# A hybrid decoder block on one core: value blocks read out behind the next split, and a bias operand of 128 rows instead of 48

## The chip, the cores and the metric

The kernel runs on one core of a Trainium2 chip. The metric is device time in microseconds (us) of one execution; lower is better. Unless marked ns, every time below is in us. A core has TensorE (matmuls, and weight loads that overlap them), VectorE, ScalarE, GpSimd and SyncE; the last one here issues most of the loads. In rows of the profile they are called PE (its weight loads PEld), DVE, ACT, POOL and SP. L454 is line 454 of the kernel before.

## The reference, cut to what matters

One layer, 256 tokens, width 2048, float32. The input is normalised to h and multiplied by one wide weight matrix `w_in`; four branches (causal pooling, dilated window attention, gated linear attention, cross-attention into 256 memory tokens) work on slices of the product. Sigmoid gates of the same product weigh the branches, and a projection with a norm and a residual ends the layer.

```
h = rms_norm(x, g_pre)
proj = h @ w_in                               # 2048 x 19472
(a_val, a_gate, sq, sk, sv, s_gate, cq, ck, cv, c_gate, c_lr,
 mq, m_gate, g_logits) = split(proj)
y_a = pool_mixer(a_val, a_gate, ...)
y_b = swa_mixer(sq, sk, sv, s_gate)
y_c = gla_mixer(cq, ck, cv, c_lr, c_gate, ...)   # gated linear attention
y_m = mem_attn(mq, m_gate, mem, ...)
gates = sigmoid(g_logits.reshape(B, S, 4, 2048) + b_merge)
merged = sum over the branches b of gates[:, :, b] * (y_b @ w_br_b)
x = x + rms_norm(merged @ w_out, g_post)
```

Two pieces of this are touched. `cv` (1024 columns) together with `c_lr` (16 columns) is the value projection of the linear attention. `b_merge` (4 x 2048) is the bias of the gates.

## The kernel before, in words

**Products in three matmuls.** Each float32 operand is split into a high half (rounded to fp32r) and a low half (the remainder). `split_w` (L149 to L154) does it for a stretch of weights: ScalarE copies the raw weights into the high tile (L152), VectorE subtracts to get the low tile (L153). `mm3` (L156 to L160) then multiplies high by high, high by low and low by high. TensorE therefore waits for both engines at the start of a stretch, and ScalarE comes first.

**Blocks.** `b_unit` computes 128 output columns of a projection, `a_block` up to 512 columns for both halves of the tokens. An `a_block` takes two accumulators in PSUM, walks four units of weights (each a DMA by SyncE into a raw buffer, L146, then one or two splits and their matmuls), and returns `finish`, which reads the two accumulators out. It has a parameter `late`: if it is given, it is called directly behind the block's first split and under `behind()`, which puts each instruction it makes behind that split on the same engine. The output projection at the kernel's end uses `late` with accumulators that alternate between two sets of buffers (`acc` and `seven`); other blocks call `finish` at once.

**The value blocks.** `cv` with `c_lr` is 1040 columns wide and done in three blocks of 348, 346 and 346 columns (`CV_BLOCKS`). All three use the set `acc`, which has two buffers: a block takes both. `cv_evac` (L546 to L554) reads them out with ScalarE copies (L550). Between one block's matmuls and the next one's stand whatever gate matmuls the gate stream puts there.

**The gate stream.** The 8192 gate columns are the kernel's largest product. `all_gates` is a generator; `gates(work)` is called after each stretch of the other blocks and advances it by as much work as was done (times 1.13), so that gate matmuls lie between the others. `gate_pair` computes 1024 of these columns with a scheme that needs fewer products. Twice in each pair an accumulation begins with `bias` (L454): one matmul whose moving operand is `brow`, 48 rows of which rows 0 to 15 hold the 16 rows of 512 bias values (high halves) and rows 32 to 47 their low halves, with zeros between. Its stationary operand is one column of `sel`, broadcast to 128 columns, that picks one row of the sixteen (or the sum of two). There are eight gate pairs and sixteen such matmuls. `bias_prep` (L434 to L451) fills `brow` and `sel` once.

**Order.** Dependencies and buffers are tracked by the framework in which the kernel is written. It also settles the order of each engine's instructions when the kernel is built, by priority (the code's order) and by what it expects to be ready; so an engine's order is not everywhere that of the code. Once built, each engine runs its list in order. `behind()` adds an edge that this ordering must keep.

Of the kernel before, what the change touches and what calls it, by code (L numbers as in the profile page):

```python
# [9 lines left out]
R = mybir.dt.float32r  # L10
AF = mybir.ActivationFunctionType
ALU = mybir.AluOpType
AX = mybir.AxisListType

P = 128
# [22 lines left out]
def kernel(ctx, tc, ins, out):  # L38
    nc = tc.nc
    ten, vec, act, pool, sync = nc.tensor, nc.vector, nc.scalar, nc.gpsimd, nc.sync  # L40

    cst = ctx.enter_context(tc.tile_pool(name="cst", bufs=1))
# [5 lines left out]
    def e8(name, shape, dt=F32):  # L48
        return big.tile(shape, dt, tag="e8", bufs=NB_E8, name=name)
# [4 lines left out]
    def c2(name, shape, dt=F32):  # L54
        return big.tile(shape, dt, tag="c2", bufs=NB_C2, name=name)
# [4 lines left out]
    def acc(name, shape):  # L60
        return ps.tile(shape, F32, tag="acc", bufs=2, name=name)

    def seven(name):
        return ps.tile([P, 512], F32, tag="seven", bufs=4, name=name)
# [13 lines left out]
    def behind():  # L78

        stack = ExitStack()  # L80
        for i in last_split:
            stack.enter_context(tc.issue_after(i))
        return stack
# [7 lines left out]
    def pull(n):  # L91
        while n > 0 and queue:
            if step(queue[0][1]):
                queue.pop(0)
            else:
                n -= 1
# [12 lines left out]
    def gates(work):  # L109
        if gate_stream[0] is None:  # L110
            return
        credit[0] += GATE_SHARE * work
        while credit[0] > 0 and gate_stream[0] is not None:
            try:
                credit[0] -= next(gate_stream[0])
            except StopIteration:
                gate_stream[0] = None
# [14 lines left out]
    ident = cst.tile([P, P], F32, name="ident")  # L132
# [11 lines left out]
    def load_raw(src, n):  # L144
        raw = new_raw()
        sync.dma_start(raw[:, :n], src[:, :n])  # L146
        return raw

    def split_w(raw_ap, n, name):  # L149
        hi = wp.tile([P, 1024], R, tag="hi", bufs=NB_HILO, name=name + "h")  # L150
        lo = wp.tile([P, 1024], R, tag="lo", bufs=NB_HILO, name=name + "l")
        last_split[0] = act.activation(hi[:, :n], raw_ap, AF.Copy).ins  # L152
        last_split[1] = vec.tensor_tensor(lo[:, :n], raw_ap, hi[:, :n].bitcast(F32), op=ALU.subtract).ins  # L153
        return hi, lo  # L154

    def mm3(o, sh, sl, wh, wl, start=False, stop=False, again=False):  # L156

        ten.matmul(o, lhsT=sh, rhs=wh, start=start, stop=False, skip_group_check=again)  # L158
        ten.matmul(o, lhsT=sh, rhs=wl, start=False, stop=False, skip_group_check=again)  # L159
        ten.matmul(o, lhsT=sl, rhs=wh, start=False, stop=stop, skip_group_check=again)  # L160

    def a_block(name, units, stat, nw, evac, load=None, per_split=None, other=False, late=None):

        accs = [seven(f"{name}a{t}") if other else acc(f"{name}a{t}", [P, 512]) for t in range(2)]
        nk = 4 * len(units)
        for u, src in enumerate(units):
            raw = load_raw(src, 4 * nw) if load is None else load(u, src)
            nk_s = max(1, 1024 // nw) if per_split is None else per_split(u)
            for hf in range(4 // nk_s):
                hi, lo = split_w(raw[:, hf * nk_s * nw : (hf + 1) * nk_s * nw], nk_s * nw, f"{name}{u}{hf}")  # L170
                if late is not None:
                    with behind():
                        late()
                    late = None
                for t in range(2):
                    ts = slice(t * P, (t + 1) * P)
                    for kk in range(nk_s):
                        k = 4 * u + nk_s * hf + kk
                        ws = slice(kk * nw, (kk + 1) * nw)
                        sh, sl = stat(k)  # L180
                        mm3(accs[t][:, :nw], sh[:, ts], sl[:, ts], hi[:, ws], lo[:, ws], k == 0, k == nk - 1)
                if hf % 2 == 0:
                    pull(1)
                gates(nk_s * 6 * (nw / 2.4 + 14) * 1e-3)
            pull(1)

        def finish():
            for t in range(2):
                evac(t, accs[t][:, :nw])

        return finish
# [5 lines left out]
    def b_unit(name, src, mov, evac, ready=None):  # L197

        a = acc(f"{name}a", [P, 512])
        if ready is None:  # L200
            raw = load_raw(src, 2048)
        for hf in range(2):
            hi, lo = ready[hf] if ready else split_w(raw[:, hf * 1024 : (hf + 1) * 1024], 1024, f"{name}{hf}")
            for kk in range(8):
                k = 8 * hf + kk
                ws = slice(kk * P, (kk + 1) * P)
                mh, _ = mov(k)
                ten.matmul(a[:], lhsT=hi[:, ws], rhs=mov.both(k), start=(k == 0), stop=False)
                ten.matmul(a[:, :T], lhsT=lo[:, ws], rhs=mh, start=False, stop=(k == KT - 1))
            if hf == 0:  # L210
                pull(1)
                gates(2.8)
        if pinned[0]:
            with behind():
                evac(name, a)
        else:
            evac(name, a)
        pull(1)
        gates(2.8)
# [30 lines left out]
    def hilo_tiles(name):  # L250
        hl = [e8(f"{name}hl{i}", [P, 4, 2, T], R) for i in range(4)]

        def at(k):
            return hl[k // 4][:, k % 4, 0, :], hl[k // 4][:, k % 4, 1, :]

        at.both = lambda k: hl[k // 4][:, k % 4]
        at.four = lambda c, i: hl[c][:, :, i, :]
        return at
# [51 lines left out]
    h_at = hilo_tiles("x")  # L310
# [114 lines left out]
        return sh[:, t * P : (t + 1) * P], sl[:, t * P : (t + 1) * P]  # L425


    brow = cst.tile([48, 512], R, name="brow")
    sel = cst.tile([48, 24], R, name="sel")

    walpha = cst.tile([16, 512], F32, name="walpha")
    big_cst = cst.tile([P, 1344], F32, name="big_cst")
# [1 line left out]
    def bias_prep():  # L434
        pool.tensor_copy(walpha[:, 0:1], xcol[0:16, 0:1])
        pool.tensor_copy(big_cst[:, 0:1], xcol[:, 0:1])
        pool.dma_start(walpha[:], ins["w_alpha"])
        pool.dma_start(big_cst[:], ins["consts"])
        raw = c2("braw", [48, 512])
        pool.memset(raw[:], 0.0)  # L440
        rows = ins["b_merge"].rearrange("b (j c) -> (b j) c", c=512)
        pool.dma_start(raw[0:16, :], rows)
        pool.dma_start(raw[32:48, :], rows)
        act.activation(brow[:], raw[:], AF.Copy)
        vec.tensor_tensor(brow[32:48, :], raw[32:48, :], brow[32:48, :].bitcast(F32), op=ALU.subtract)
        one = c2("bsel", [48, 24])
        vec.tensor_tensor(one[:, 0:16], ident[0:48, 0:16], ident[0:48, 32:48], op=ALU.add)
        two = one[:, 0:16].rearrange("p (r i) -> p r i", i=2)
        vec.tensor_tensor(one[:, 16:24], two[:, :, 0], two[:, :, 1], op=ALU.add)
        vec.tensor_copy(sel[:], one[:])  # L450
        yield  # L451

    def bias(o, r):
        ten.matmul(o, lhsT=sel[:, r : r + 1].to_broadcast([48, P]), rhs=brow[:], start=True, stop=False)  # L454

    gate_dram = {}

# [83 lines left out]
    cv = e8("cv", [P, 2, 1024])  # L541
# [4 lines left out]
    def cv_evac(j):  # L546
        def evac(t, a):
            c0, n = CV_BLOCKS[j]
            nv = min(n, 1024 - c0)
            act.activation(cv[:, t, c0 : c0 + nv], a[:, :nv], AF.Copy)  # L550
            if nv < n:
                act.activation(lr[:, t, :], a[:, nv:n], AF.Copy)

        return evac  # L554
# [136 lines left out]
    for n in range(8):  # L691
        if n == 6:
            drain("quarters")
            pinned[0] = False
            gate_stream[0] = all_gates()
        if n < 6:
            ahead[cqk[n + 1][0]] = b_split(*cqk[n + 1])
        evac = plain_evac(gq[:, n, :], SCALE) if n < 4 else plain_evac(gk[:, n - 4, :])
        b_unit(*cqk[n], h_at, evac, ahead.pop(cqk[n][0], None))
    for j in range(3):  # L700
        c0, n = CV_BLOCKS[j]
        a_block(f"cv{j}", [ins[f"w_cv{j}"][u] for u in range(4)], h_at, n, cv_evac(j))()
    queue.append(("mnorm", m_norm()))
    queue.append(("gla", gla()))
    for h in range(4):
# [109 lines left out]
    for g in (3, 2, 1, 0):  # L815
        u = c4(f"u{g}", [P, 2, PAD + T])
# [127 lines left out]
    for n, (j, i) in enumerate(order):  # L944
        name, b, nu = branches[i]
# [35 lines left out]
    late = None  # L981
    for j in range(3):
        late = a_block(f"o{j}", [ins["w_out"][j, u] for u in range(4)], o_at, 512, o_evac(j, 512 * j, 512),
                       other=j % 2 == 1, late=late)
# [5 lines left out]
    for u in range(4):  # L990
        raw = load_raw(ins["w_last"][1, u], 1024)
# [104 lines left out]
```

## Time and profile before

| what | value |
|---|---|
| three runs | 1174.86 median, 1171.3 to 1175.29 |
| the profiled execution | 1172.68, of which its span 1170.6 |
| clock granted to TensorE | 0.998 of full speed |
| HBM | 285.11 MB read, 17.83 MB written, 259 GB/s over the span |
| gate weight loads (`in_w_g`) | 112 loads of 1024 KB, median 5.8 from issue to landing |
| value block loads (`in_w_cv`) | 12 loads, 3.9 to 6.9 from issue to landing |

A row of the timeline gives start, duration, engine, line, operation, output <- inputs and count; in brackets stand the idle time of the engine just before it and what ended that. Matmuls are pipelined, so a matmul's duration is longer than its share of TensorE's time: the step from one start to the next is what it takes. A row of the waits gives who waited for whom, in total, how often, and the longest. A row of one line's instructions gives minimum, median and maximum duration in ns and the first and last start. A row of groups gives the count, then busy time in us and the mean of one in ns, then the idle time before.

### The profile page before, as it was taken

To read this page: it belongs to the slowest core of one execution; us is meant where nothing else is said; L and a number is where in the kernel's file an instruction comes from. 1 tells how busy PE (TensorE), PEld (TensorE's weight loads), DVE (VectorE), ACT (ScalarE), POOL (GpSimd) and SP (SyncE) were. 2 spreads that over 40 slices of the span, in tenths; PEclk is the share of its full clock that TensorE was granted. 3 is DMA by queue.
4 is the path that set the end of the run, shared out by engine and by line. 5 is a ranking of instruction groups with operands and counts; after the bars stand their busy time and mean duration, and the time that the engine had idled before them with its cause. 6 is when DMAs were issued, how large, how long until landed. Compare 5 with 4: busy or idle time off the path is not lost.

```text
span 1170.6 us, 15411 instructions
## 1 busy us (share of the span) xinstructions
PE 1149.8 (98%) x5854; PEld 968.2 (83%) x5854; DVE 961.2 (82%) x1201; ACT 647.0 (55%) x823; POOL 59.0 (5%) x109
## 2 busy tenths in 40 slices
PE   9999999999999999999999999999999999999997
PEld 7887898878888888878888887888788888888887
DVE  7979798999898799889989988987898676777454
ACT  7656456665655555665566556566555543434441
POOL 0010000000101001000000000000000102110000
PEclk9999999999999999999999999999999999999999
DMA  9755679757868688777788777876778988759321
GB/s 356 316 182 193 217 251 343 277 203 281 304 238 284 217 297 289 259 251 263 276 295 315 251 263 271 294 253 231 272 252 303 372 308 306 252 206 381 118 73 73
DMA packets 79946, 303.94 MB, mean 260 GB/s; under 512 B 6224, under 2 KB 8656, under 8 KB 57344
## 3 DMA queue, kind: packets, MB, share of 16 engines
q1 hardware_dynamic: 65568, 268.45, 63.5%
q0 software_dynamic: 8976, 24.91, 6.1%
q10 hardware_dynamic: 5328, 9.60, 2.2%
q8 instruction: 46, 0.75, 0.3%
q14 instruction: 28, 0.23, 0.1%
HBM read 285.11 MB, written 17.83 MB: 259 GB/s over the span
## 4 chain that ended last, share of the span: by engine, by line
PE 76%; DVE 5%; DMA 3%; ACT 2%; issue 2%; DVEq 0%; POOLq 0%; POOL 0%; ACTq 0%
PE q L158 5%; PE q L159 5%; PE q L160 5%; DMA raw<-in_w_g 2%; PE p L158 2%; PE p L159 1%; PE p L160 1%; PE sv2a L159 1%; PE sv0a L158 1%; PE sv0a L160 1%; PE o0a L160 1%; PE sv2a L158 1%; PE o0a L158 1%; PE sv1a L158 1%; PE sv0a L159 1%
## 5 line engine op out<-in xcount | busy, mean ns | idle before, releaser
L491 DVE TENSOR_TENSOR raw<-raw 128x1024 f32<-128x1024 f32 x64 | 78.1, 1220 | 8.9 <-DMA raw<-in_w_g 8.9
L497 DVE TENSOR_TENSOR raw<-raw 128x512 f32<-128x512 f32 x64 | 44.5, 696 | 1.1
L492 DVE TENSOR_TENSOR raw<-raw 128x512 f32<-128x512 f32 x64 | 44.5, 697 | 0.5
L918 POOL DMA_DIRECT2D g<-gd x32 | 17.4, 554 | 98.6 <-DVE merged L926 66.7
L926 DVE TENSOR_TENSOR merged<-merged,g 128x512 f32<-128x512 f32 x24 | 15.5, 686 | 0.0
L710 POOL DMA_DIRECT2D cgd<-cgate x4 | 2.2, 552 | 201.7 <-DVE cgate L241 201.7
L885 POOL DMA_DIRECT2D ybd<-ybt x4 | 2.7, 678 | 174.1 <-DVE ybt L247 174.1
L853 PE MATMUL sp<-k,q 128*128 128x128 f32 (+1 forms) x48 | 10.2, 335 | 1.0 <-DVE k L226 1.0
L861 ACT ACTIVATE s<-s,st 128x384 f32<-128x384 f32 (+1 forms) x8 | 6.2, 769 | 6.7 <-DVE st L860 6.7
L853 PEld LDWEIGHTS sp<-k,q 128*128 128x128 f32 x48 | 7.4, 190 | 2.9 <-DVE k L226 1.4
L856 DVE SCALAR_TENSOR_TENSOR s<-big_cst,sp 128x128 f32<-128x128 f32 (+1 forms) x24 | 7.1, 349 | 2.0 <-PE sp L853 2.0
L246 ACT ACTIVATE xhl<-xn 128x1024 fp32r<-128x1024 f32 x4 | 4.2, 1060 | 7.0 <-DVE xn L330 7.0
L459 ACT ACTIVATE c<-c 128x512 f32<-128x512 f32 x8 | 5.0, 628 | 5.5 <-DVE c L505 3.9
L939 ACT ACTIVATE mTh<-mtp 128x512 fp32r<-128x512 f32 x8 | 4.3, 595 | 6.3 <-PE mtp L937 6.3
L459 ACT ACTIVATE c<-p 128x512 f32<-128x512 f32 x8 | 4.7, 587 | 5.1 <-PE p L160 5.1
L664 POOL TENSOR_TENSOR ms<-ms,half 128x2 f32<-128x2 f32 x4 | 5.7, 1428 | 35.2 <-DVE ms L663 35.2
L879 PE MATMUL po<-pt,sv 128*128 128x256 f32 x24 | 7.2, 384 | 0.2 <-ACT pt L874 0.2
L812 POOL DMA_DIRECT2D yad<-yat x4 | 2.7, 686 | 88.5 <-DVE yat L247 88.5
L360 DVE SCALAR_TENSOR_TENSOR mhl<-mr,vecs,mhl 128x256 fp32r<-128x256 f32 x16 | 6.8, 479 | 0.4 <-issue 0.3
L652 POOL TENSOR_TENSOR sq<-sq 128x256 f32<-128x256 f32 x4 | 4.4, 1106 | 53.0 <-ACT sq L651 53.0
L359 ACT ACTIVATE mhl<-mr,vecs 128x256 fp32r<-128x256 f32 x16 | 6.9, 495 | 0.2 <-DMA mr<-in_memT 0.2
L1003 POOL TENSOR_TENSOR opart<-opart,half 128x1 f32<-128x1 f32 x2 | 1.1, 562 | 116.0 <-DVE opart L1002 116.0
(4603 smaller groups left out, 4582.7 us busy)
## 6 DMA issues: line engine op xcount, KB each, us to landing
raw<-in_w_g SPq DMA_DIRECT2D x112, 1024.0 KB, 5.8
raw<-in_w_sqk SPq DMA_DIRECT2D x24, 1024.0 KB, 6.6
raw<-in_w_sv SPq DMA_DIRECT2D x12, 1024.0 KB, 6.5
raw<-in_w_out SPq DMA_DIRECT2D x12, 1024.0 KB, 9.6
raw<-in_w_cqk SPq DMA_DIRECT2D x8, 1024.0 KB, 15.0
raw<-in_w_cg SPq DMA_DIRECT2D x8, 1024.0 KB, 6.6
raw<-in_w_av SPq DMA_DIRECT2D x8, 1024.0 KB, 5.0
raw<-in_w_ag SPq DMA_DIRECT2D x8, 1024.0 KB, 6.0
```

Of the source, the lines that this page charges most:

```text
L158: ten.matmul(o, lhsT=sh, rhs=wh, start=start, stop=False, skip_group_check=again)
L159: ten.matmul(o, lhsT=sh, rhs=wl, start=False, stop=False, skip_group_check=again)
L160: ten.matmul(o, lhsT=sl, rhs=wh, start=False, stop=stop, skip_group_check=again)
L459: act.activation(dst, src, AF.Tanh, scale=0.5)
L491: vec.tensor_tensor(r4[:, :, 0, :], r4[:, :, 0, :], r4[:, 1, :, :], op=ALU.add)
L492: vec.tensor_tensor(r4[:, 1, 1, :], r4[:, 1, 1, :], r4[:, 0, 0, :], op=ALU.add)
L497: vec.tensor_tensor(r4[:, 0, 1, :], r4[:, 0, 1, :], r4[:, 1, 1, :], op=ALU.add)
L853: ten.matmul(parts[g], lhsT=q3[:, g, it * P : (it + 1) * P], rhs=k3[:, g, :nj], start=True, stop=True)
L856: vec.scalar_tensor_tensor(s[:, g, :], dist[:, g, :], SLOPES[g * 4 + hh], parts[g], op0=ALU.mult, op1=ALU.add)
L879: ten.matmul(po[:], lhsT=sv[g][:, 0, vs], rhs=pt[g][:, 0:T], start=(g == 0), stop=False)
L918: pool.dma_start(gs[t][:], gate_dram[b, j, t][:])
L926: vec.tensor_tensor(m, m, gs[t][:], op=ALU.add)
```

## The change

Two parts. The `finish` of a value block is no longer called at once: it goes into the next block as `late`, and so stands behind that block's first split on ScalarE; the third one's is called behind the loop. The tiles of the bias grow from 48 to 128 partitions; rows 48 to 127 are zero, and the bias matmul has 128 rows.

```
-    brow = cst.tile([48, 512], R, name="brow")
-    sel = cst.tile([48, 24], R, name="sel")
+    brow = cst.tile([P, 512], R, name="brow")
+    sel = cst.tile([P, 24], R, name="sel")
...
-        raw = c2("braw", [48, 512])
+        raw = c2("braw", [P, 512])
         pool.memset(raw[:], 0.0)
...
-        one = c2("bsel", [48, 24])
-        vec.tensor_tensor(one[:, 0:16], ident[0:48, 0:16], ident[0:48, 32:48], op=ALU.add)
+        one = c2("bsel", [P, 24])
+        vec.tensor_tensor(one[:, 0:16], ident[:, 0:16], ident[:, 32:48], op=ALU.add)
...
     def bias(o, r):
-        ten.matmul(o, lhsT=sel[:, r : r + 1].to_broadcast([48, P]), rhs=brow[:], start=True, stop=False)
+        ten.matmul(o, lhsT=sel[:, r : r + 1].to_broadcast([P, P]), rhs=brow[:], start=True, stop=False)
...
+    late = None
     for j in range(3):
         c0, n = CV_BLOCKS[j]
-        a_block(f"cv{j}", [ins[f"w_cv{j}"][u] for u in range(4)], h_at, n, cv_evac(j))()
+        late = a_block(f"cv{j}", [ins[f"w_cv{j}"][u] for u in range(4)], h_at, n, cv_evac(j), late=late)
+    late()
```

## Prediction

> **What bounds the kernel now.** I read the engines' busy times and the chain that ended last first.
>
> ```profile
> PE 1149.8 (98%) x5854; PEld 968.2 (83%) x5854; DVE 961.2 (82%) x1201; ACT 647.0 (55%) x823; POOL 59.0 (5%) x109
> PE 76%; DVE 5%; DMA 3%; ACT 2%; issue 2%; DVEq 0%; POOLq 0%; POOL 0%; ACTq 0%
> ```
>
> TensorE is busy for 98% of the span and carries three quarters of the chain. Only two things can shorten this kernel: an idle stretch of TensorE that goes, or a matmul that takes less of TensorE's time. The change tries one of each, so the next view is who TensorE waits for (in total, how often, the longest).
>
> ```profile
> PE p L158 <- ACT p1c L480: 2.4, 4, 0.9
> PE cv1a L158 <- ACT cv100h L152: 1.2, 1, 1.2
> PE p L159 <- DVE gu2100l L153: 0.6, 1, 0.6
> PE cv1a L159 <- DVE cv100l L153: 0.3, 1, 0.3
> ```
>
> The longest single wait is the start of the second value block, and the DVE wait that follows it belongs to the same place. Idle time is one thing; a busy TensorE can also be slow. So I then looked at the timeline around the bias matmuls, because a step from one start to the next shows what a matmul really takes.
>
> ```profile
> 607.51 0.39 PE L159 MATMUL q<-gv0131l,quarter 128*128 128x512 f32 x1
> 607.74 0.39 PE L160 MATMUL q<-gv0131h,quarter 128*128 128x512 f32 x1
> 608.06 0.50 PE L454 MATMUL p<-brow,sel 48*128 48x512 f32 x1
> 608.49 0.50 PE L158 MATMUL p<-gu1100h,xhl 128*128 128x512 f32 x1
> 608.83 0.40 PE L159 MATMUL p<-gu1100l,xhl 128*128 128x512 f32 x1
> ```
>
> Two ordinary matmuls of 512 columns start 0.23 apart (607.51 to 607.74). Around the bias the steps are 0.32, 0.43 and 0.34. The bias starts late, its successor starts late, and so does the one after.
>
> **First part: the value blocks read out behind the next split.** The seam between the first and the second value block, in the timeline of ScalarE, of VectorE and of TensorE:
>
> ```profile
> 139.66 0.46 ACT L550 ACTIVATE cv<-cv0a 128x348 f32<-128x348 f32 x1 [5.11 <-PE cv0a L160]
> 140.60 0.46 ACT L550 ACTIVATE cv<-cv0a 128x348 f32<-128x348 f32 x1 [0.48 <-PE cv0a L160]
> 140.96 0.77 ACT L152 ACTIVATE cv100h<-raw 128x692 fp32r<-128x692 f32 x1
> ```
>
> ```profile
> 141.76 0.88 DVE L153 TENSOR_TENSOR cv100l<-raw,cv100h 128x692 fp32r<-128x692 f32 x1 [5.66 <-ACT cv100h L152]
> ```
>
> ```profile
> 140.09 0.32 PE L159 MATMUL cv0a<-cv031l,xhl 128*128 128x348 f32 x1
> 140.25 0.32 PE L160 MATMUL cv0a<-cv031h,xhl 128*128 128x348 f32 x1
> 141.78 0.59 PE L158 MATMUL cv1a<-cv100h,xhl 128*128 128x346 f32 x2 [1.22 <-ACT cv100h L152]
> 142.70 0.42 PE L159 MATMUL cv1a<-cv100l,xhl 128*128 128x346 f32 x1 [0.33 <-DVE cv100l L153]
> ```
>
> ScalarE waited 5.11 for the block's sums, copied both accumulators, and only then began the split that TensorE needs. VectorE had nothing for 5.66. The change moves that split (one ACT instruction of 0.77) ahead of the two copies; nothing is added or removed, and the load of the split's data is issued where it was. So the question is when the data is there: the issue in SyncE's timeline, and the DMA list of this stretch with the median time to landing.
>
> ```profile
> 135.34 1.12 SPq L146 DMA_DIRECT2D raw<-in_w_cv  x2
> ```
>
> ```profile
> raw<-in_w_cv SPq DMA_DIRECT2D x2, 692.0 KB, 4.5
> ```
>
> The first of these two loads goes out at 135.34; with the 4.5 median to landing it is there at about 139.8 (an estimate). The split then starts 1.1 earlier than 140.96. Its low half starts at about 140.65 instead of 141.76, and the first product with that half at about 141.6 instead of 142.70. An earlier landing gives up to the time at which the old block itself ends. The matmul that starts at 142.70 is the third after the one at 140.25, and with no wait it would come at 140.25 + 3 x 0.16 = 140.73 with no wait, so the seam can give back at most 1.97. (0.16 is the step from 140.09 to 140.25.) I take 1.4, nearer to what the landing allows, and keep 0 and 2.0 as ends.
>
> What comes late next? The accumulators. All three blocks use the same two, so the first matmul of the second block now waits for a copy that stands behind the split: 139.8 + 0.77 + 0.46 = 141.0, still before the low half is ready. The second copy can't start before 140.60, as now, and ends at 141.06; its matmuls come after six others. So this wait stays hidden, by some tenths. On ScalarE the splits of the block's second half and of the gate weights are queued behind the waiting copies. They are now queued there as well, and VectorE, which works without a break afterwards, moves forward with the first low half.
>
> The second seam shows the asked-for order already, because the instruction order is settled when the kernel is built and need not be the code's:
>
> ```profile
> 163.00 0.77 ACT L152 ACTIVATE cv200h<-raw 128x692 fp32r<-128x692 f32 x1
> 163.68 0.44 ACT L550 ACTIVATE cv<-cv1a 128x346 f32<-128x346 f32 x1
> 164.01 0.77 ACT L152 ACTIVATE cv201h<-raw 128x692 fp32r<-128x692 f32 x1
> ```
>
> ```profile
> 163.88 0.32 PE L160 MATMUL cv1a<-cv131h,xhl 128*128 128x346 f32 x1
> 164.04 0.39 PE L158 MATMUL q<-gt006ah,quarter 128*128 128x512 f32 x1
> ...
> 166.76 0.32 PE L158 MATMUL cv2a<-cv200h,xhl 128*128 128x346 f32 x1
> ```
>
> Split, copy, split; TensorE goes straight on with a gate's matmuls (starts 0.16 apart, then 0.23). Nothing is to be had there: 0. The third block is read out directly behind the loop, where it was: 0.
>
> **Second part: 128 rows for the bias.** Sixteen bias matmuls:
>
> ```profile
> L454 PE MATMUL p<-brow,sel x8: 492/497/498, 84.0 to 806.1; 48*128 48x512 f32 x8
> L454 PE MATMUL q<-brow,sel x8: 385/490/498, 84.4 to 808.3; 48*128 48x512 f32 x8
> ```
>
> The single one above takes from 607.74 to 608.83 = 1.09 for three steps, against 3 x 0.23 = 0.69: 0.40 too much. Ten stand alone; six come as three pairs, of which this is the first:
>
> ```profile
> 83.80 0.28 PE L209 MATMUL ck0a<-xhl,ck01l 128*128 128x256 f32 x1
> 84.02 0.50 PE L454 MATMUL p<-brow,sel 48*128 48x512 f32 x1
> 84.36 0.39 PE L454 MATMUL q<-brow,sel 48*128 48x512 f32 x1
> 84.67 0.50 PE L208 MATMUL ck1a<-xhl,ck10h 128*128 128x512 f32 x1
> 85.01 0.28 PE L209 MATMUL ck1a<-xhl,ck10l 128*128 128x256 f32 x1
> 85.12 0.40 PE L208 MATMUL ck1a<-xhl,ck10h 128*128 128x512 f32 x1
> ```
>
> From 83.80 to 85.01 are 1.21; undisturbed it would be 0.11 (85.01 to 85.12) + 3 x 0.23 = 0.80. So a pair costs 0.41 together: the price is paid on going to 48 rows and on coming back, not by each bias. Thirteen places at 0.40 make 5.2. With 128 rows the bias is a matmul like its neighbours, so I put it at their 0.23.
>
> Where TensorE waits for someone else right behind the bias, the gain only lengthens that wait. That is so at four places: two pairs, behind which these rows stand (the first of TensorE, the second of its weight loads),
>
> ```profile
> 395.01 0.50 PE L158 MATMUL p<-gu3000h,xhl 128*128 128x512 f32 x1 [0.37 <-ACT gu3000h L152]
> 500.93 0.19 PEld L158 LDWEIGHTS p<-gu0100h,xhl 128*128 128x128 f32 x1 [0.37 <-ACT gu0100h L152]
> ```
>
> and two single ones just ahead of the wait for gu2100l in the list of waits. For these I take 0.4 of 1.6. The other nine give 9 x 0.40 = 3.6. So this part is worth 4.0, with ends 0 and 5.2; a loss here is excluded by the neighbours, which have 128 rows and the shorter step.
>
> The Trainium skill speaks against this part: in "TensorE: Matmul & The Clock Gate", "Why this matters for your kernels", a single matmul over 32 partitions takes the same time as one over 128. By that rule the sum would hold the first part alone. The trace disagrees as far as a sequence goes (steps of 0.32, 0.43 and 0.34 against 0.23). The skill's "TensorEngine Tiling (Array Packing)", "Key Properties", has a rule that a change of tiling mode drains the array, which would put the excess at the change of row count, as the pair does; no run so far shows whether 48 rows are such a mode.
>
> The preparation runs once: zeroing, a copy on ScalarE, a few VectorE instructions, each with as many elements per partition as before. The nearest row for a full-height copy is
>
> ```profile
> L459 ACT ACTIVATE c<-p 128x512 f32<-128x512 f32 x8 | 4.7, 587 | 5.1 <-PE p L160 5.1
> ```
>
> 0.59, in time hidden under TensorE's running matmuls ahead of 84.0. Cost 0; without that cover a tenth or two.
>
> **The sum.** 1.4 + 4.0 = 5.4. Somewhat less reaches the end, since VectorE at 82% is close behind TensorE and some later waits will grow; I take off 0.2. The profiled execution took 1172.68 (span 1170.6 and 2.1 around it), so it would take 1167.5. That execution is 2.2 below the median of the three runs, 1174.86; on the median the forecast is 1174.86 - 5.2 = 1169.7.
>
> **The rivals.** *Everything passes through.* The load lands early, all thirteen places count, and later waits don't grow: 2.0 + 5.2 = 7.2, so 1167.7 on the median. For it: VectorE still has 18% idle, so it can follow. Against it: the four places with a wait behind them.
>
> *The bias gains nothing*, because the late starts come from something other than the row count (the broadcast stationary operand, which stays). Then the first part alone remains: 1174.86 - 1.4 = 1173.5. For it: only the bias rows have this operand, so the trace can't part the two. Against it: its weight load is as long as the others (0.18 and 0.19), and the matmul behind the bias is disturbed too, though its own operand is ordinary.
>
> *Slower: the late copies hold the accumulators.* The order is settled anew at build, and the copies may be put behind the next gate's splits as well as behind the block's own. At the first seam these are the two of gt004, of which this is the second, in ScalarE's timeline:
>
> ```profile
> 146.34 1.04 ACT L152 ACTIVATE gt004bh<-raw 128x1024 fp32r<-128x1024 f32 x1
> ```
>
> It is done at 147.4; a copy of 0.46 behind it ends at 147.9, and the second block would start 6.1 after its present 141.78. The second seam has no cover left once its gate matmuls are through, and could lose as much: 12.2 less the bias's 4.0 is 8.2 slower, 1183.1. It decides once the first copy starts later than 141.3 (141.78 less 0.46). Against it: the second seam has each copy between the block's own two splits.
>
> **How the numbers follow.** A measurement of this kernel tells about 0.5%, or 5.9, from no change. The forecast gets 0.48; its own spread, 4 to 6.2, reaches over that bound a little, so 0.07 of it counts as faster and 0.41 as same. Everything passing through gets 0.33, faster. The bias without gain gets 0.14, same. The accumulators held get 0.05, slower. That makes 0.40, 0.55 and 0.05. The range reaches from the full gain on the profiled execution (1172.68 - 7.2 = 1165.5) up to the first part alone (1173.5), and leaves out the slower case and some of the edges.
>
> **What would show it.** Right: the bias's rows read 128*128 128x512 with steps of 0.23 on both sides; its mean is near 0.40 instead of 0.50; the two waits of cv1a are gone from TensorE's list or below 0.5 together; ScalarE has cv100h ahead of both copies; the span is near 1165.4. Wrong: steps of 0.3 and more around a 128-row bias; cv1a waiting for a copy at L550; or the other waits in TensorE's list grown by as much as these fell.

## The result, and the profile after

| | before | after |
|---|---|---|
| median of four runs each | 1174.38 | 1165.85 |
| profiled execution, and its span | 1172.68, 1170.6 | 1165.77, 1163.7 |
| ratio, with its 95% interval | | 0.9932 [0.9913, 0.9951] |

The changed kernel is faster by 0.7%. The forecast was 1169.7 with a range from 1165.5 to 1173.5: the time lies at the lower end of it, 1.8 below the rival in which everything passes through (1167.7). Part of that distance is the kernel before: its median here is 1174.38, and in two later sets of runs 1171.99 (12 runs) and 1172.45 (25 runs). The two traces, 1170.6 and 1163.7, differ by 6.9, and this is the gain that is explained below.

Busy times of the changed kernel:

```profile
PE 1143.3 (98%) x5854; PEld 968.3 (83%) x5854; DVE 961.0 (83%) x1201; ACT 647.6 (56%) x823; POOL 58.8 (5%) x109
```

The same number of matmuls takes 6.5 less of TensorE's time, and the span fell by 6.9. So the time in which TensorE is idle fell by 0.4 only (20.8 to 20.4). The seam's two waits, 1.2 and 0.3, are gone from its list, but others grew, as that for gu2100l from 0.6 to 1.4, and a new one of 0.9 came. The two groups of bias rows, and one place in TensorE's timeline that answers to the one shown before:

```profile
L454 PE MATMUL p<-brow,sel x8: 391/395/477, 83.8 to 800.9; 128*128 128x512 f32 x8
L454 PE MATMUL q<-brow,sel x8: 387/436/580, 84.1 to 802.7; 128*128 128x512 f32 x8
```

```profile
604.00 0.39 PE L160 MATMUL q<-gv0131h,quarter 128*128 128x512 f32 x1
604.22 0.39 PE L454 MATMUL p<-brow,sel 128*128 128x512 f32 x1
604.45 0.40 PE L158 MATMUL p<-gu1100h,xhl 128*128 128x512 f32 x1
604.68 0.39 PE L159 MATMUL p<-gu1100l,xhl 128*128 128x512 f32 x1
```

The steps are 0.22, 0.23 and 0.23, where they were 0.32, 0.43 and 0.34. Not every place looks so: two biases of the second group still read 0.58. At four single ones (196.0, 293.5, 310.8 and 802.7), each behind a matmul of another branch with 2 to 256 columns, the step behind the bias is 0.31 to 0.42. The step ahead of it is then only 0.03 to 0.11, so the three steps together are 0.62 to 0.75, where they were 0.94 to 1.08. The gain there is 0.29 to 0.40.

The seam between the first two value blocks, in the timelines of ScalarE, VectorE and TensorE:

```profile
133.96 0.76 ACT L152 ACTIVATE cv100h<-raw 128x692 fp32r<-128x692 f32 x1
135.53 0.79 ACT L152 ACTIVATE cv101h<-raw 128x692 fp32r<-128x692 f32 x1 [0.81 <-PE cv0a L160]
139.18 0.46 ACT L550 ACTIVATE cv<-cv0a 128x348 f32<-128x348 f32 x1 [2.86 <-PE cv0a L160]
140.12 0.46 ACT L550 ACTIVATE cv<-cv0a 128x348 f32<-128x348 f32 x1 [0.48 <-PE cv0a L160]
```

```profile
135.53 0.87 DVE L153 TENSOR_TENSOR cv100l<-raw,cv100h 128x692 fp32r<-128x692 f32 x1
```

```profile
139.77 0.32 PE L160 MATMUL cv0a<-cv031h,xhl 128*128 128x348 f32 x1
139.93 0.32 PE L158 MATMUL cv1a<-cv100h,xhl 128*128 128x346 f32 x1
140.09 0.32 PE L159 MATMUL cv1a<-cv100l,xhl 128*128 128x346 f32 x1
```

Both splits of the second block's first unit stand ahead of both copies, and the first one's two halves were done (136.40) more than three microseconds before TensorE needed them. TensorE goes from the first block to the second without a step longer than 0.16. The first copy ends at 139.64, before the second block's first matmul, and the second one stays hidden as well.

**Where the 6.9 came from.** Each matmul of the kernel after was set beside the same one before. The lead (start before less start after) is level over long stretches and changes at few places. The table gives those changes in order of time; they are differences of median starts in the two traces, and add up to 6.88. In all the lead grows from 0.07 behind the start-up to 6.91 at the end, by 6.84; small steps back make the rest.

| place (time before) | what stands there | lead |
|---|---|---|
| 84 | pair of biases | +0.41 |
| 141 to 148 | first seam, and the gate matmuls behind it | +2.92 |
| 181 | a wait of 0.17 for VectorE's sum q (L509), in the third value block, gone | +0.26 |
| 191, 200 | two biases | +0.66 |
| 200 to 240 | the wait for c at 211.9 (-1.17), behind a gate load, below; small ones near 237 | -1.49 |
| 297, 314 | two biases | +0.62 |
| 394, 501 | two pairs of biases with a wait behind | 0 |
| 411 | wait for p1c | +0.34 |
| 608, 625 | two biases | +0.84 |
| 702 to 721 | two biases (+0.92), the wait for gu2100l (-0.77), a later wait | +0.52 |
| 807, 809 | two biases | +0.55 |
| 832 to 835 | gt310's waits, gone | +1.25 |

### The profile page after: what moved, and what is told of

Same layout as the page of the kernel before. It is cut to its first block, busy times and chain, and to the rows that moved or that the text cites. A ratio compares the mean times of both kernels' runs of the same rounds, so it can differ in the third digit from the quotient of the medians.

```text
span 1163.7 us, 15411 instructions
## 1 busy us (share of the span) xinstructions
PE 1143.3 (98%) x5854; PEld 968.3 (83%) x5854; DVE 961.0 (83%) x1201; ACT 647.6 (56%) x823; POOL 58.8 (5%) x109
## 4 chain that ended last, share of the span: by engine, by line
PE 87%; DVE 6%; DMA 3%; issue 2%; ACT 2%; SPq 0%; DVEq 0%; POOLq 0%; POOL 0%; ACTq 0%
PE q L158 6%; PE q L159 6%; PE q L160 6%; PE p L158 2%; PE p L159 2%; PE p L160 2%; DMA raw<-in_w_km 1%; PE kma L387 1%; PE sv2a L159 1%; PE sv0a L158 1%; DMA gd<-c 1%; PE sv0a L160 1%; PE o0a L158 1%; PE sv0a L159 1%; PE sv2a L160 1%
```

## The experiments

Times of different runs were taken beside runs of the kernel before, in sets on different chips, and each ratio is to the runs of its own set; so runs of different sets are compared by ratio. Spans of single profiles differ by up to some 2 in the first 60 microseconds alone, whatever the kernel (the lead of the run without the bias, below, falls by 2.2 there); so differences of one microsecond between two spans are read from medians or from the place in the trace, not from the spans.

### Each part alone

The late read-out with 48 rows (the changed kernel, with the bias's lines as they were before):

```
-    brow = cst.tile([P, 512], R, name="brow")
+    brow = cst.tile([48, 512], R, name="brow")
...
```

> The read-out of the value blocks behind the next split alone; the bias keeps its 48 rows. Theory A (the two parts are independent and the seam is worth what TensorE lost there): the first seam gives back about 2.0 at once and 2.9 by the time the block's gate matmuls are done, so the span is 1168 to 1169 against 1170.6, and the bias rows still read 48 rows with starts 0.32, 0.43 and 0.34 apart. Rival B (the seam's gain is lost again at later waits, the whole of the result is the bias): the span stays within 0.7 of 1170.6. Rival C (the seam is most of the result and the bias little): 1165 or less.

Measured: 1168.68, ratio 0.9969 [0.9957, 0.9981], span 1167.2. And the bias over 128 rows with the read-out at once:

```
-        late = a_block(f"cv{j}", [ins[f"w_cv{j}"][u] for u in range(4)], h_at, n, cv_evac(j), late=late)
-    late()
+        a_block(f"cv{j}", [ins[f"w_cv{j}"][u] for u in range(4)], h_at, n, cv_evac(j))()
```

> The bias over 128 rows alone; the value blocks are read out at once. Theory A: nine to thirteen places at 0.40, a span of 1165.4 to 1167.0 against 1170.6, and the seam's two waits of 1.2 and 0.3 still there. Rival B (all of the result is the bias): 1163.7. Rival C (the seam is most of it): 1169 or more.

Measured: 1169.45, ratio 0.9978 [0.9967, 0.9989], span 1167.7. Both parts gain by themselves; neither is the whole. The two ratios together make 0.9947, inside the interval of the change, 0.9913 to 0.9951. So theory A holds for the independence. Its sizes do not: both spans lie outside what it had, the seam's part is larger (3.4 by span) and the bias's smaller (2.9). In the first run the lead jumps by 2.9 at the seam, as in the changed kernel; in the second the seam's two waits stand unchanged:

```profile
PE cv1a L158 <- ACT cv100h L152: 1.2, 1, 1.2
PE cv1a L159 <- DVE cv100l L153: 0.3, 1, 0.3
```

### What makes a bias matmul dear

Into each step of the gates' scheme of the changed kernel goes one more matmul, 64 in all, whose stationary operand is zero, over K rows (K stands for 128, 96, 64, 48 and 32):

```
+            ten.matmul(q7[:], lhsT=sel[0:K, 24:25].to_broadcast([K, P]), rhs=brow[0:K, :], start=False, stop=sp)
```

> The changed kernel with 64 more matmuls, one in each step of the gates' scheme, 128 rows by 512 columns with a stationary operand of zeros: the base line for the same matmul over fewer rows. All theories: 64 at 0.23, 14.7 longer than the changed kernel, a span of about 1178.4.

> The 64 added matmuls over 96 rows. Theory T (the price is that of a change to an array mode of at most 64 rows): like 128 rows, a span of about 1178.4. Theory P (any row count other than its neighbours' costs): 64 at 0.40 more, about 1204, some of it hidden where TensorE waits anyway.

> The 64 added matmuls over 64 rows. Theories T and P both: 64 at 0.40 more than over 128 rows, about 1204; if only a count that is no power of two is dear (theory O): about 1178.4.

> The 64 added matmuls over 48 rows, the row count that the bias had. All of T, P and O: 64 at 0.40 more than over 128 rows, about 1204. Near 1178.4 would say that the row count is not the cause.

> The 64 added matmuls over 32 rows. T and P: about 1204 as with 48 and 64 rows; a rival by which the price goes with the number of rows that are missing would put it above them (0.40 x 96/80 = 0.48 each, about 1209) and 96 rows at 0.16 each (about 1189).

Each was run once.

| rows | span | span over that of 128 rows, divided by 64 | three steps at the added matmul, median of 64 |
|---|---|---|---|
| 128 | 1177.9 | | 0.693 |
| 96 | 1179.8 | 0.03 | 0.698 |
| 64 | 1205.7 | 0.43 | 1.086 |
| 48 | 1202.8 | 0.39 | 1.086 |
| 32 | 1207.0 | 0.45 | 1.088 |

The three steps run from the start of the matmul ahead to the start of the second one behind, as in the prediction. TensorE's timeline at one of the 64, with 96 rows and with 48:

```profile
477.23 0.39 PE L160 MATMUL q<-gt306ah,quarter 128*128 128x512 f32 x1
477.46 0.40 PE L497 MATMUL q<-brow,sel 96*128 96x512 f32 x1
477.69 0.40 PE L158 MATMUL q<-gt306ah,quarter 128*128 128x512 f32 x1
477.93 0.40 PE L159 MATMUL q<-gt306al,quarter 128*128 128x512 f32 x1
```

```profile
489.03 0.39 PE L160 MATMUL q<-gt306ah,quarter 128*128 128x512 f32 x1
489.35 0.50 PE L497 MATMUL q<-brow,sel 48*128 48x512 f32 x1
489.78 0.50 PE L158 MATMUL q<-gt306ah,quarter 128*128 128x512 f32 x1
490.11 0.40 PE L159 MATMUL q<-gt306al,quarter 128*128 128x512 f32 x1
```

Theory T's numbers hold by the steps: the price is 0.393 (1.086 less 0.693), the same within 0.002 for 32, 48 and 64 rows, and 96 rows pay 0.005. So it does not grow with the number of missing rows, it is not peculiar to counts that are no power of two, and it is not the broadcast operand, which all five have. Nothing between 64 and 96 rows was run. 64 x 0.393 = 25.2, and the span with 48 rows is longer by 24.9; that these are so close is partly luck, since the spans of the 64 and 32 rows are another 3 to 4 longer at the same steps. Part of that is later waits: the longest, that of attention's scores `sp` for `k`, is 2.3 with 48 rows, 3.3 with 64 and 3.4 with 32.

The weight loads show what goes with the price. With 96 rows, then with 48, the loads of the added matmul and of the one behind it:

```profile
477.24 0.19 PEld L497 LDWEIGHTS q<-brow,sel 96*128 96x128 f32 x1
477.46 0.19 PEld L158 LDWEIGHTS q<-gt306ah,quarter 128*128 128x128 f32 x1
```

```profile
489.35 0.18 PEld L497 LDWEIGHTS q<-brow,sel 48*128 48x128 f32 x1 [0.35 <-issue]
489.77 0.19 PEld L158 LDWEIGHTS q<-gt306ah,quarter 128*128 128x128 f32 x1 [0.24 <-issue]
```

With 96 rows each load starts with the matmul ahead of its own, 0.22 to 0.23 early, and is hidden under it. With 48 rows both start together with their own matmul (489.35 and 489.78). So two loads, 0.18 and 0.19, are no longer hidden; together they are 0.37 of the 0.393. All 64 places of the runs with 64, 48 and 32 rows show this, and none with 96 or 128. That the lost cover is the whole price was not tested by itself.

The Trainium skill's "TensorEngine Tiling (Array Packing)", "Available Configurations" and "Key Properties", names array modes of 128, 64 and 32 rows and says that changing the mode drains the array. These runs fit that and put a number on it: 0.393 for going down and coming back. The rule of the Trainium skill's "TensorE: Matmul & The Clock Gate", "Why this matters for your kernels", that a single matmul over 32 partitions takes the same time as one over 128 does not carry over to one that stands among full ones (three steps of 1.088 against 0.693).

### The same at another line

Linear attention's gate has 16-row matmuls of its own. The changed kernel, with these over 128 rows, the added rows zeroed in both tiles:

```
-    walpha = cst.tile([16, 512], F32, name="walpha")
+    walpha = cst.tile([P, 512], F32, name="walpha")
...
-        lrT = c2("lrT", [16, T])
-        vec.tensor_copy(lrT[:], plr[:])
+        lrT = c2("lrT", [P, T])
+        pool.memset(lrT[:], 0.0)
+        vec.tensor_copy(lrT[0:16, :], plr[:])
```

> The changed kernel, with the 16-row matmuls of linear attention's gate (8 records in two groups) over 128 rows as well, the added rows zero. If going from 128 to fewer rows and back costs 0.40 wherever it is done, the two groups give 0.8: a span of 1162.9 against 1163.7, and the rows of that line stand as far apart as other 128-row matmuls of this kind (0.22). If the price is peculiar to the bias matmul, the span stays at 1163.7 within 0.2.

Measured: 1165.37, ratio 0.994 [0.9928, 0.9953], span 1163.8. Nothing to be seen against the changed kernel (0.9932, 1163.7); by the span alone this is the outcome that was expected of a price peculiar to the bias. The place itself decides. The two groups stand as one in the trace, so there was one place, not two. In the changed kernel:

```profile
222.56 0.28 PE L209 MATMUL cg10a<-xhl,cg101l 128*128 128x256 f32 x1
222.77 1.99 PE L573 MATMUL pz<-lrT,walpha 16*128 16x256 f32 x8
224.69 0.50 PE L158 MATMUL q<-gt102ah,quarter 128*128 128x512 f32 x1
225.03 0.40 PE L159 MATMUL q<-gt102al,quarter 128*128 128x512 f32 x1
```

From 222.56 to 225.03 are 2.47; with 128 rows the same stretch took 2.07 (221.03 to 223.10). The 0.40 is there, and it is gone again further on: behind this place the run leads the changed kernel by 1.92 (1.1 of it from the wait at 208 of the next section but one, which it does not have), and it loses 0.62 at 234, 0.66 at 716 and 0.29 at 828, which leaves 0.23.

### Who has to be ahead of the read-out

The bias-alone kernel, with the copies of the read-out on VectorE:

```
-            act.activation(cv[:, t, c0 : c0 + nv], a[:, :nv], AF.Copy)
+            vec.tensor_copy(cv[:, t, c0 : c0 + nv], a[:, :nv])
```

> Bias over 128 rows, value blocks read out at once as before, but the read-out's copies of the value columns run on VectorE instead of ScalarE. ScalarE is then free to split ahead of the block's end; VectorE has the copies ahead of the low half. Theory A (both engines of the split must be ahead of the read-out): the step from the last product of the first block to the first low product of the second, 2.45 before, falls by about 0.7 only, to 1.7 to 1.8, and the span is about 1167.0 against 1167.7 for the bias alone. Rival B (it is enough that ScalarE is free): that step falls by 2.0 to about 0.5, and the span is 1165 or less.

Measured: 1170.02, ratio 0.9975 [0.9963, 0.9986], span 1166.2. VectorE's timeline, then TensorE's:

```profile
138.65 0.52 DVE L550 COPY cv<-cv0a 128x348 f32<-128x348 f32 x1 [3.58 <-PE cv0a L160]
139.60 0.52 DVE L550 COPY cv<-cv0a 128x348 f32<-128x348 f32 x1 [0.42 <-PE cv0a L160]
140.04 0.87 DVE L153 TENSOR_TENSOR cv100l<-raw,cv100h 128x692 fp32r<-128x692 f32 x1
```

```profile
139.25 0.32 PE L160 MATMUL cv0a<-cv031h,xhl 128*128 128x348 f32 x1
139.40 0.32 PE L158 MATMUL cv1a<-cv100h,xhl 128*128 128x346 f32 x1
140.17 0.42 PE L158 MATMUL cv1a<-cv100h,xhl 128*128 128x346 f32 x1 [0.45 <-DVE cv L550]
140.96 0.43 PE L159 MATMUL cv1a<-cv100l,xhl 128*128 128x346 f32 x1 [0.37 <-DVE cv100l L153]
```

ScalarE split early here too, at 133.42. The low half waited behind the copies. From the last product of the first block to the first low product are 1.71, where before had 2.45 and the changed kernel has 0.32. Theory A holds: both engines of the split must stand ahead of the read-out. Part of the 1.71 is another wait, 0.45 for the second copy, because this build has the second accumulator's first product so early; the low product's own wait comes last there (0.37). The ratio is no better than with the bias alone (0.9978).

### What gives gains back between 200 and 240

VectorE is busy for 43.65 of the 45 from 200 to 245 in the run with the late read-out alone. The theory was that it bounds this stretch. Two of its instructions there were left out (linear attention's cumulative sum and a difference, their tiles filled by GpSimd with constants), with 48 and with 128 rows:

```
-        vec.tensor_tensor_scan(bc[:].rearrange(...), scan_m[:].rearrange(...), z[:].rearrange(...), 0.0, ALU.mult, ALU.add)
+        pool.memset(bc[:], -0.5)
...
-        vec.tensor_tensor(kd[:], bc[:, :, CHUNK - 1 : CHUNK].to_broadcast([P, 16, CHUNK]), bc[:], op=ALU.subtract)
+        pool.memset(kd[:], -0.25)
```

> Late read-out, bias of 48 rows, and two VectorE instructions of the stretch from 200 to 245 left out (linear attention's cumulative sum and the difference behind it, their tiles filled with constants by GpSimd; some 3.5 of VectorE's time). It is the base line for the next run. VectorE is busy for 43.65 of these 45 in the run with the late read-out alone. If it bounds the stretch, the span falls by 0.5 to 1.5 against that run's 1167.2; if not, it stays.

> As the run before, with the bias over 128 rows. Theory V (VectorE's stretch takes part of the bias's gain): the difference between these two is larger than the 3.5 between the late read-out alone (1167.2) and the changed kernel (1163.7), 3.9 to 4.6, and the lead of this kernel over the other does not shrink between 200 and 245. Rival: 3.5 or less, with the lead shrinking there as it does without the two instructions left out.

Measured: 1169.79, ratio 0.998 [0.9971, 0.9988], and 1167.67, ratio 0.9963 [0.9948, 0.9977]; spans 1167.8 and 1168.1. The first is no faster than with the two instructions in (0.9969), the two differ by 2.1 and not by 3.9 to 4.6, and the lead of the second over the first shrinks by 1.9 near 208 all the same. So what theory V expected did not come.

The two runs are no clean test of it, though. The cumulative sum stands at 237.06 in the changed kernel, behind the place where most of the lead goes. And with its tiles filled early, ScalarE takes two exponentials (L594 and L603) ahead of a gate's split, so that both runs have a new wait:

```profile
234.35 0.73 PE L158 MATMUL q<-gt103ah,quarter 128*128 128x512 f32 x2 [1.42 <-ACT gt103ah L152]
```

What speaks against theory V at the place itself is that VectorE has idle time there. It waits for a load. VectorE's timeline before, after, and in the run with 128 rows and without the two instructions:

```profile
200.51 1.23 DVE L491 TENSOR_TENSOR raw<-raw 128x1024 f32<-128x1024 f32 x1
```

```profile
198.46 1.23 DVE L491 TENSOR_TENSOR raw<-raw 128x1024 f32<-128x1024 f32 x1 [1.94 <-DMA raw<-in_w_g]
```

```profile
200.26 1.22 DVE L491 TENSOR_TENSOR raw<-raw 128x1024 f32<-128x1024 f32 x1 [2.34 <-DMA raw<-in_w_g]
```

Before, the gate weights were there when VectorE came to them. After, their load goes out 3.7 earlier (191.15 instead of 194.86), but takes 7.2 to land instead of 5.6, and VectorE waits. From there on VectorE is ahead of the kernel before by 2.05, where TensorE is ahead by 4.33. ScalarE's read-out of a gate, c, stands behind VectorE's work, and TensorE needs it. ScalarE and TensorE before, then after:

```profile
210.06 0.58 ACT L459 ACTIVATE c<-p 128x512 f32<-128x512 f32 x1
211.89 0.40 PE L158 MATMUL q<-gt100bh,xhl 128*128 128x512 f32 x1
```

```profile
208.00 0.58 ACT L459 ACTIVATE c<-p 128x512 f32<-128x512 f32 x1
208.64 0.50 PE L158 MATMUL q<-gt100bh,xhl 128*128 128x512 f32 x1 [0.92 <-ACT c L459]
```

c comes 2.06 earlier, as VectorE does. Before, it was ready 1.25 ahead of TensorE (210.64 against 211.89); TensorE, now 4.33 ahead, waits for it. This is read from the traces; no run with that load moved was made, so it is not shown by experiment.

### The bias left out

The changed kernel without its sixteen bias matmuls (the gates lack `b_merge`):

```
-        bias(p1[:], 4 * b + j0)
...
-        bias(q5[:], 16 + 2 * b + jj)
```

> The changed kernel with the sixteen bias matmuls left out (the gates lack b_merge). Sixteen at 0.23 are 3.7: if all of TensorE's time passes through, a span of 1160.0 against 1163.7. If the places ahead of a stretch that another engine bounds (two ahead of 200 to 245, three places around 390, 500 and 700) give theirs back, half of it: 1161.0 to 1162.0.

Measured: 1166.76, ratio 0.9957 [0.9938, 0.9976], six runs from 1164.09 to 1171.09. What was expected did not come: the ratio is no better than that of the changed kernel (0.9932), though 3.7 of TensorE's work is missing, and the shortest of the six spans is 1162.0. It is no clean test: the order of instructions changed as well, and the profile (the longest of the six, span 1169.0) had lost 2.2 by 60 microseconds. So it leaves open what the bias still costs. In its trace the largest wait is

```profile
PE p L158 <- ACT p1c L480: 3.4, 4, 2.0
```

against 2.1 in the changed kernel.

## Why the prediction was right, and where its sizes were not

**The direction and both mechanisms held.** TensorE was the bound, the seam's wait went, the biases' late starts went, and the range held the time, by 0.35 at its lower end. That it did is partly luck. The forecast was built on the median of three runs, 1174.86, which is over 2 above the kernel's later medians, and the lower end on the profiled execution, 1172.68; from the median the full gain of 7.2 would have ended at 1167.7 and missed. By the traces 6.9 came where 5.2 was forecast. The chances put the result with "same"; it came out as faster by more than 0.5%. The terms missed by +1.5 (seam), -0.8 (bias) and +0.9 (later waits).

**First part: 1.4 forecast, 2.9 found at the seam.** The step that was off was the landing of the data. The prediction took the first of the two loads issued at 135.34 for the one that the split needs. A block has four units and so four loads; these two are the sixth and seventh of the twelve, the second block's second and third unit. The split needs the fifth:

```profile
127.47 0.33 SPq L146 DMA_DIRECT2D raw<-in_w_cv  x1
```

It landed 3.9 later, at 131.4, long before ScalarE's copies. (Nor was it issued where it had been: after the change it goes out at 121.58.) And in the kernel after, ScalarE splits at 133.96, before the two loads that answer to the ones at 135.34 go out (134.85 and 135.64). So nothing but the order on ScalarE held the split, and the seam gave back its whole bound: the low product comes 0.32 after the block's last one instead of 2.45 (the third matmul behind that last one comes 0.48 later instead of 2.45: 1.97 less, the end that the prediction kept). The rest of the 2.9 came from a step that the prediction had at nothing: TensorE waited behind the block for a gate's split too, before the change.

```profile
147.43 0.50 PE L158 MATMUL q<-gt004bh,quarter 128*128 128x512 f32 x1 [0.21 <-ACT gt004bh L152]
```

The lead grows by 0.8 at gt004's first matmuls, because the two splitting engines moved forward by more than TensorE did (ScalarE began this split at 141.43 instead of 146.34).

The cover of the copies held with more to spare than worked out (the first ended at 139.64, before it was needed). The second seam was worth 0, as its rows said. The slower rival's point, a first copy starting after 141.3, was not reached: it started at 139.18.

**Second part: 4.0 forecast, about 3.2 in the table, 2.9 alone.** The price of 0.40 was right among full matmuls (0.40 at 608 and 625, 0.393 by the 64 added ones), and it is the row count's. Taken for every place it was a little high: over three steps the nine places without a wait behind them gained 0.29 to 0.40, and they gave 3.08 in the table for 3.6 forecast. Of the four with a wait the two pairs gave 0 and the two single ones 0.92 less 0.77, against 0.4 forecast. The rival in which the bias gains nothing is refuted by the steps of 0.23 with the broadcast operand in place. One of the prediction's signs of being wrong, steps of 0.3 and more around a 128-row bias, did show at a few places; the sum of the three steps says that the price is gone there too.

**The allowance for later waits: 0.2 taken off, 0.7 gained.** The table holds -1.49 between 200 and 240 and +1.25 near 833, with smaller ones (+0.26, +0.34 and +0.37, the last at the later wait near 721). Their sum has the other sign than the prediction's. That it is small is chance: the two large ones lie behind waits for single gate loads. Ahead of 833 VectorE waited 2.27 for one before the change and 0.95 after.

## What to carry to other kernels

Read a matmul's price from the steps between starts on both sides of it, not from its own duration: here the matmul behind the one with few rows paid as well. A matmul over 64 rows or fewer among full ones can be cheaper over 128 rows with zeros; the gain comes once for a group of such matmuls (0.41 for a pair, 0.40 for a group of eight), not for each. Over 96 rows there was nothing to gain. Where a block's read-out waits for its last product, put both engines' share of the next split ahead of it, and before pricing such a move find out which load feeds the split.

## What was not expected of the hardware

A matmul over 96 rows costs as much as one over 128 (0.698 against 0.693 for three steps), and one over 32 as much extra as one over 64 (0.395 and 0.393 more). The price goes with two weight loads that no longer hide under the matmul ahead: they start 0.002 ahead of their own matmul instead of 0.231. And a gain of some tenths on the bounding engine can vanish at a load: VectorE waited 0 for one load before and 1.94 after, and TensorE's lead shrank by 1.17 a few microseconds later.
